# A float32 projection of the memory rows, and S5's input maps in three wide operations

## The chip, the cores and the metric

The kernel runs on one core of one Trainium2 chip. The metric is device time in microseconds (us) for one execution. Inputs, weights and outputs are float32 in HBM.

## What is computed

One inference step of a two-layer hybrid encoder, for a prompt of 512 tokens and a sample of 32 tokens, side by side as 544 columns of feature-major activations. Only the part around the change matters here:

```python
# memory rows, for both layers: 256 rows of width 1024
m = rms_norm(mem[None], mem_norm_g[:, None, None, :])
kv = jnp.einsum('lbmd,ldk->lbmk', m, w_mem_kv)          # (2 layers, 256 rows, 512)
k, v = jnp.split(kv, 2, axis=-1)
k = rms_norm(k.reshape(...), mem_k_norm_g[...])
# S5 (layer 0): discretised input matrix, then a complex diagonal recurrence per state
bb_re = f_re[..., None] * b_re - f_im[..., None] * b_im
bb_im = f_re[..., None] * b_im + f_im[..., None] * b_re
bu_re = jnp.einsum('blgc,gnc->blgn', ug, bb_re)
bu_im = jnp.einsum('blgc,gnc->blgn', ug, bb_im)
h_t = lam * h_(t-1) + bu_t                               # complex, by an associative scan
y = einsum(h_re, c_re) - einsum(h_im, c_im) + d_skip * u
```

Layer 0 then mixes S5 (with a gated linear unit, GLU) and attention into the memory rows, and a wide feed-forward network follows. Layer 1 has latent attention, memory attention and a second feed-forward network.

## The kernel before

**Matrix products.** Most products run in three terms of the reduced type fp32r: a float32 operand is split into a high part and a remainder, and hi*hi, hi*lo and lo*hi are summed in PSUM. `weights` makes the split of a weight block: SyncE's queue loads it into a slot `wraw` (three slots), ScalarE copies it to `whi` (L231) and its negative to `wlo` (L232), and a DMA issued by GpSimd adds the block from HBM onto `wlo` (L233). The activations are split by ScalarE (the copy) and VectorE (the remainder).

**Order.** The program is written in one order with a priority for each part (`ORDER`), and a planner, which runs a model of the engines, lays every engine's instructions out in a fixed order. A changed instruction can so move others.

**The stage of the change.** After the first product of layer 0 (`z0`, eight blocks, L324) the loop over `m` in 0..5 does S5 for eight groups of states at a time. In each turn:

- `s5_scan` (L752 to L782): products of the inputs with the maps `wv`, then the recurrence on VectorE;
- `s5_input` (L729 to L740): transposes of the next inputs, copied by ScalarE;
- `s5_wv` (L669, L672), in `products`: the input maps of the next `m`, on VectorE; `s5_wvt` (L681, L683), in `turn`: their transposes on TensorE and the copies on ScalarE;
- `s5_wc` (L694 to L710) and `s5_kernel` (L719): the output maps, and the short convolution kernel, which goes to DRAM (`kd`) and back by DMAs that GpSimd issues;
- `s5_output` (L791 to L805): true float32 products, transposes, and the activation.

`s5_wv` works on a real and an imaginary part. For each part it makes two products of 512 columns (L669) and one sum or difference of 512 (L672): six operations for each `m`.

**Memory rows.** `mem_kv` is a generator whose units the loop inserts with `fill` (priority `mem_kv`, -60: late). Eight units (four pairs of feature blocks, two layers) each scale and split two feature blocks (L344, L345), get a split weight block by `weights` from `w_mkv`, and issue twelve fp32r products of 128x512 (L350). The units after them make rms norms and transposes (L367 to L406) and stand at priority 580.

**Parameters of S5.** `s5_params` makes the powers `pr`, `pi` of the decay (L613 to L618), `bb` (L626 to L629), and by ScalarE the layouts `prd` (L654) and `xq` (L656).

Of the kernel before, what the change touches and what calls it, by code (L numbers as in the profile page):

```python
# [18 lines left out]
KD = D // 128  # L19
# [49 lines left out]
def view(a, dims, off=0):  # L69
    a = a[:]  # L70
    return bass.AP(tensor=a.tensor, offset=a.offset + off, ap=[a.ap[0]] + [list(d) for d in dims])
# [66 lines left out]
def body(ctx, tc, A, O):  # L138
# [7 lines left out]
    def slots(pool, n, dt, w, name):  # L146
        return Slots([pool.tile([128, w], dt, name=f"{name}{i}") for i in range(n)])
# [58 lines left out]
    def gcol(name, i):  # L206
        c = GP[name] + i
        return gp[:, c:c + 1]
# [18 lines left out]
    def weights(ap, *n, lo_eng=None):  # L227

        raw, hi, lo = WR.get(*n), WH.get(*n), WL.get(*n)
        nc.sync.dma_start(raw, ap)  # L230
        S.activation(hi, raw, AF.Copy)  # L231
        S.activation(lo, raw, AF.Copy, scale=-1.0)  # L232
        P.dma_start(lo, ap, accum_op=ALU.add)  # L233
        WR.put(raw)
        return hi, lo
# [8 lines left out]
    def wfree(w):  # L244
        WH.put(w[0])
        WL.put(w[1])
# [79 lines left out]
    def combos(a, b):  # L326
        return ((a[0], b[0]), (a[0], b[1]), (a[1], b[0]))
# [6 lines left out]
    def mem_kv(fm, rm, bm, b1, dst):  # L334
        ps = [[bm.get(512) for _ in range(2)] for _ in range(2)]
        acc = fm.get(2, NMEM)
        for u in range(4):
            mt = fm.get(2, NMEM)
            nc.sync.dma_start(mt, A["mem"][:, 2 * u:2 * u + 2, :])
            for l in range(2):  # L340
                hi, lo = rm.get(2, NMEM), rm.get(2, NMEM)
                for k2 in range(2):
                    g = gcol("mem", l * KD + 2 * u + k2)
                    S.activation(hi[:, k2], mt[:, k2], AF.Copy, scale=g)  # L344
                    V.scalar_tensor_tensor(lo[:, k2], mt[:, k2], g, hi[:, k2].bitcast(F32), ALU.mult, ALU.subtract)  # L345
                w = weights(A["w_mkv"][l, u], 1024, lo_eng=V if l else P)
                for t in range(2):
                    for k2 in range(2):
                        for i, (x, ww) in enumerate(combos((hi, lo), w)):
                            T.matmul(ps[l][t], x[:, k2, 128 * t:128 * t + 128], ww[:, 512 * k2:512 * k2 + 512],  # L350
                                     start=u == 0 and k2 == 0 and i == 0, stop=u == 3 and k2 == 1 and i == 2)
                wfree(w)
                rm.put(hi, lo)
                if l:
                    if u:
                        q = fm.get(2, NMEM)
                        S.activation(q, mt, AF.Square)
                        P.tensor_tensor(acc, acc, q, ALU.add)
                        fm.put(q)
                    else:  # L360
                        S.activation(acc, mt, AF.Square)
                    fm.put(mt)
                yield
        b = b1.get(512)
        for t in range(2):
            for u in range(2):
                T.matmul(b[:, t:t + 1], acc[:, u, 128 * t:128 * t + 128], ones, start=u == 0, stop=u == 1)  # L367
        x = sm(2, "mx", 1)
        V.tensor_scalar(x, b[:, :2], 1.0 / D, EPS, ALU.mult, ALU.add)
        b1.put(b)  # L370
        fm.put(acc)
        r = rsqrt(x, 128, 2, "mrs")
        yield
        for l in range(2):
            kt, v = dst[l]
            ss = sm(8, "mss")
            q = fm.get(2, 256)
            for t in range(2):
                S.activation(q[:, t], ps[l][t][:, :256], AF.Square, scale=r[:, t:t + 1])
                S.activation(v[:, t, :], ps[l][t][:, 256:], AF.Copy, scale=r[:, t:t + 1])  # L380
            V.tensor_reduce(ss, view(q, [[64, 8], [1, 64]]), AX.X, ALU.add)
            P.dma_start(O["mem_v"][l].rearrange("t p c -> p t c"), v)
            yield
            x = sm(8, "mkx")
            V.tensor_scalar(x, ss, 1.0 / 64, EPS, ALU.mult, ALU.add)
            y = rsqrt(x, 128, 8, "mkr")
            fm.put(q)
            V.tensor_tensor(y.rearrange("p (t h) -> p t h", t=2), y.rearrange("p (t h) -> p t h", t=2),
                            view(r, [[1, 2], [0, 4]]), ALU.mult)
            yield  # L390
            kk = fm.get(2, 256)
            for t in range(2):
                V.tensor_tensor(kk[:, t].rearrange("p (h d) -> p h d", d=64),
                                ps[l][t][:, :256].rearrange("p (h d) -> p h d", d=64),
                                view(y, [[1, 4], [0, 64]], 4 * t), ALU.mult)
            bm.put(*ps[l])
            kf = view(kk, [[64, 8], [1, 64]])
            V.tensor_tensor(kf, kf, view(grow(f"mk{l}"), [[0, 8], [1, 64]]), ALU.mult)
            P.dma_start(O["mem_k"][l].rearrange("t p c -> p t c"), kk)
            yield  # L400
            pt = b1.get(512)
            for hp in range(2):
                for t in range(2):
                    T.transpose(pt[:, 256 * hp + 128 * t:256 * hp + 128 * t + 128],
                                kk[:, t, 128 * hp:128 * hp + 128], ident)
            S.activation(kt.rearrange("p a b -> p (a b)"), pt, AF.Copy, scale=mqg[:, l:l + 1])  # L406
            b1.put(pt)
            fm.put(kk)
            yield
# [136 lines left out]

    def s5_params(pool, tmp, sp5):
        q = {}
        bb = pool.tile([128, 2, NPR, 16], F32, name="bb2")
        cc = pool.tile([128, 2, 48, 16], F32, name="cc2")  # L550
        braw = tmp[:, :2 * NPR * 16].rearrange("p (a b c) -> p a b c", a=2, b=NPR)
        nc.sync.dma_start(braw, A["s5b"])
# [67 lines left out]
        cm(3, 2, 2, 1)  # L620
        cm(5, 4, 4, 1)

        x, y = bb[:, 0], bb[:, 1]
        t = tmp[:, H:2 * H].rearrange("p (a b c) -> p a b c", a=2, b=NPR)
        frb, fib = view(fr, [[0, 2], [1, NPR], [0, 16]]), view(fi, [[0, 2], [1, NPR], [0, 16]])
        V.tensor_tensor(bb, braw, frb, ALU.mult)  # L626
        V.tensor_tensor(t, braw, fib, ALU.mult)
        V.tensor_tensor(x, x, t[:, 1], ALU.subtract)
        V.tensor_tensor(y, y, t[:, 0], ALU.add)  # L629

        tab = pool.tile([128, 2, NPR, 70], F32, name="tab")
        V.memset(tab[:, 0, :, 0:1], 1.0)
# [16 lines left out]
        for half in range(2):  # L649
            a = slice(64 * half, 64 * half + 64)  # L650
            for gh in range(2):
                c = slice(64 * gh, 64 * gh + 64)
                for i, src in enumerate((pr, pi)):
                    S.activation(view(prd[a], [[48, 9], [8, NM], [1, 4]], 432 * i + 4 * gh),  # L654
                                 view(src[c], [[NPR, 9], [4, NM], [1, 4]]), AF.Copy)
                S.activation(view(xq[a], [[128, NM], [1, 64]], 64 * gh),  # L656
                             view(bb[c], [[64, NM], [1, 64]], 16 * NPR * half), AF.Copy)
        q.update(pr=pr, pi=pi, bb=bb, cc=cc, tab=tab, prd=prd, xq=xq)
        q["kp"] = pool.tile([128, 2, 240], F32, name="kp")
        P.memset(q["kp"], 0.0)  # L660
        q["hf"] = pool.tile([128, NM, 8, 2], F32, name="hf")
# [1 line left out]

    def s5_wv(q, m, fa, fb):

        a, b = fa.get(2, 4, 128), fb.get(2, 4, 128)
        for ri in range(2):
            for o, x, pw in ((a, ri, "pr"), (b, 1 - ri, "pi")):
                V.tensor_tensor(o[:, ri].rearrange("p i (s c) -> p i s c", s=8),  # L669
                                view(q["bb"], [[16, 4], [0, 8], [1, 16]], 16 * (NPR * x + 4 * m)),  # L670
                                view(q[pw], [[1, 4], [NPR, 8], [0, 16]], 4 * m), ALU.mult)
            V.tensor_tensor(a[:, ri], a[:, ri], b[:, ri], ALU.add if ri else ALU.subtract)  # L672
        fb.put(b)
        return a

    def s5_wvt(a, fs, fd, bs):
        wv = []
        for ri in range(2):
            pb = bs.get(512)
            for i in range(4):  # L680
                T.transpose(pb[:, 128 * i:128 * i + 128], a[:, ri, i], ident)  # L681
            w = fs.get(4, 128)
            S.activation(w.rearrange("p a b -> p (a b)"), pb, AF.Copy)  # L683
            bs.put(pb)
            wv.append(w)
        fd.put(a)
        return wv
# [313 lines left out]
    exr.close()  # L1001
    exr = ExitStack()
    lr = exr.enter_context(tc.tile_pool(name="l0b", bufs=1, reuse_waits="tile"))
    R, fx = slots(lr, 4, F32R, 512, "rb"), slots(lr, 3, F32, FW, "fx")
    FA, FB, FD = slots(lr, 2, F32, 1024, "wv"), slots(lr, 1, F32, 2 * FW, "tb"), slots(lr, 3, F32, 2 * FW, "wc")
    fxs = list(fx.free)
    F.merge(fx)
# [793 lines left out]
```

## Time and profile before

| | |
|---|---|
| three runs | 1451.24, 1451.76, 1459.61 us (median 1451.76) |
| profiled execution | 1449.85 us, of which span 1448.1 us |
| busy share of the span | TensorE 97%, VectorE 50%, ScalarE 52%, GpSimd 27% |
| mean granted TensorE clock | 0.985 of full |

The span is the time from the first to the last instruction that the profiler records. Matmuls overlap in the pipeline and their ends are modelled, so the step from one start to the next, not the duration, is the price of a matmul; the same goes for VectorE, where an operation begins before the one ahead has drained. In an engine's timeline the brackets give the idle time ahead of an instruction and what ended it. The two shares say little of the change: the stage that it touches lasts about a tenth of the span.

### The profile page before, as it was taken

The numbers are of one execution on the slowest core, as the hardware profiler recorded it, in microseconds if no ns is written. First come the engines' busy times: TensorE is split into PE (matmuls) and PEld (weight loads), VectorE is DVE, ScalarE is ACT, GpSimd is POOL, SyncE is SP. The second block draws the span as 40 slices with busy tenths as digits, with TensorE's granted clock in tenths as the row PEclk, the third lists the DMA queues.
The fourth block names the chain that finished last, engine by engine and source line by source line (L and its number), as shares of the span: only waits on it lengthen the run. The fifth ranks groups of instructions, "written<-read, shape, count | busy, mean of one in ns | idle before, by whom it ended". The sixth has DMA issues, their size and how long they took to land.

```text
span 1448.1 us, 26899 instructions
## 1 busy us (share of the span) xinstructions
PE 1403.1 (97%) x10693; PEld 1310.7 (91%) x10693; DVE 723.6 (50%) x1810; ACT 755.9 (52%) x1247; POOL 388.6 (27%) x676
## 2 busy tenths in 40 slices
PE   7978799999999999999989999999999999999998
PEld 6966689999999999999988987557999999999998
DVE  7989742455514551455257655663355513551351
ACT  6656555565535553556555554654555534553452
POOL 2155432322111211124325421432322211221121
PEclk8999889999999999999999999999999999999999
DMA  9754637778788888869742432002778887888875
GB/s 268 163 142 121 155 75 175 169 164 175 176 179 171 176 176 178 173 141 207 158 120 62 124 102 60 11 20 57 165 171 177 177 175 172 176 177 174 176 157 139
DMA packets 67198, 214.80 MB, mean 148 GB/s; under 512 B 9280, under 2 KB 11552, under 8 KB 67072
## 3 DMA queue, kind: packets, MB, share of 16 engines
q0 software_dynamic: 30304, 100.81, 38.5%
q1 hardware_dynamic: 35616, 110.17, 26.5%
q10 hardware_dynamic: 1152, 2.10, 0.4%
q8 instruction: 84, 1.38, 0.4%
q14 instruction: 42, 0.34, 0.1%
HBM read 207.41 MB, written 5.61 MB: 147 GB/s over the span
## 4 chain that ended last, share of the span: by engine, by line
PE 82%; DVE 2%; DMA 2%; ACT 2%; issue 2%; POOL 1%; DVEq 0%; POOLq 0%; ACTq 0%
PE bank L324 64%; PE bank L1308 2%; PE bank L1556 2%; PE bank L1395 2%; PE bank L1592 1%; PE bank L1509 1%; PE bank L1483 1%; PE bank L1581 1%; DMA wlo<-i_w_f 1%; PE bank L1197 1%; PE bank L482 1%; PE bank L520 1%; PE bank L1423 1%; PE bank L510 0%; PE bank L1364 0%
## 5 line engine op out<-in xcount | busy, mean ns | idle before, releaser
L324 PE MATMUL bank<-rc,whi 128*128 128x272 f32 x3728 | 628.9, 290 | 0.2 <-DVE rc L305 0.2
L324 PEld LDWEIGHTS bank<-rc,whi 128*128 128x128 f32 x3728 | 530.3, 189 | 5.3 <-issue 4.3
L324 PE MATMUL bank<-rc,wlo 128*128 128x272 f32 x1864 | 389.4, 289 | 0.0
L231 ACT ACTIVATE whi<-wraw 128x1024 fp32r<-128x1024 f32 (+2 forms) x186 | 191.5, 1029 | 360.1 <-issue 311.3
L324 PEld LDWEIGHTS bank<-rc,wlo 128*128 128x128 f32 x1864 | 294.0, 189 | 0.4 <-issue 0.2
L324 PE MATMUL bank<-g,whi 128*128 128x272 f32 x1408 | 234.6, 288 | 0.8 <-ACT g L216 0.8
L324 PEld LDWEIGHTS bank<-g,whi 128*128 128x128 f32 x1408 | 198.8, 188 | 1.3 <-ACT g L216 1.2
L233 POOL DMA_DIRECT2D wlo<-i_w_f x136 | 117.5, 864 | 303.8 <-ACT wlo L232 300.5
L232 ACT ACTIVATE wlo<-wraw 128x1024 fp32r<-128x1024 f32 (+2 forms) x186 | 189.1, 1017 | 3.9 <-PE bank L350 3.3
L324 PE MATMUL bank<-g,wlo 128*128 128x272 f32 x704 | 145.8, 288 | 1.8 <-DMA wlo<-i_w_f 1.6
L851 DVE SCALAR_TENSOR_TENSOR fa<-fa,gp,fa 128x546 f32<-128x546 f32 x88 | 69.7, 792 | 139.8 <-ACT fa L850 139.8
L865 DVE TENSOR_TENSOR h<-bank,h 128x272 f32<-128x272 f32 x96 | 38.2, 436 | 172.3 <-PE bank L324 171.9
L324 PEld LDWEIGHTS bank<-g,wlo 128*128 128x128 f32 x704 | 110.4, 188 | 2.2 <-DMA wlo<-i_w_f 2.2
L850 ACT ACTIVATE fa<-fa,gp 128x546 f32<-128x546 f32 x88 | 73.2, 832 | 12.8 <-DVE fa L845 12.8
L843 DVE TENSOR_TENSOR fa<-bank,fa 128x272 f32<-128x272 f32 x88 | 38.9, 443 | 81.7 <-PE bank L324 77.5
L852 DVE SCALAR_TENSOR_TENSOR fa<-fa,gp,fa 128x546 f32<-128x546 f32 x88 | 69.5, 790 | 3.1
L891 ACT ACTIVATE fa<-fa 128x546 f32<-128x546 f32 x44 | 29.2, 663 | 71.7 <-DVE fa L852 71.7
L847 POOL COPY fa<-gp 128x2 f32<-128x2 f32 x88 | 19.0, 216 | 168.3 <-DVE g L217 107.7
L848 POOL COPY fa<-fa 128x4 f32<-128x4 f32 x88 | 18.2, 207 | 165.2 <-DVE fa L845 165.2
L324 PE MATMUL bank<-ra,whi 128*128 128x272 f32 x256 | 47.5, 307 | 3.1 <-ACT whi L241 3.1
L216 ACT ACTIVATE g<-fa 128x544 fp32r<-128x544 f32 x44 | 29.0, 659 | 37.6 <-DVE fa L893 37.6
L892 DVE TENSOR_TENSOR fa<-fa,fa 128x512 f32<-128x512 f32 x44 | 30.5, 693 | 33.6 <-ACT fa L891 33.6
(629 smaller groups left out, 2020.3 us busy)
## 6 DMA issues: line engine op xcount, KB each, us to landing
wraw<-i_w_f SPq DMA_DIRECT2D x120, 512.0 KB, 4.9
wlo<-i_w_f POOLq DMA_DIRECT2D x120, 512.0 KB, 7.4
wraw<-i_w_out SPq DMA_DIRECT2D x16, 512.0 KB, 4.3
wlo<-i_w_out POOLq DMA_DIRECT2D x16, 512.0 KB, 7.1
wraw<-i_w_in SPq DMA_DIRECT2D x14, 512.0 KB, 5.0
wlo<-i_w_in POOLq DMA_DIRECT2D x14, 512.0 KB, 7.7
wraw<-i_w_f SPq DMA_DIRECT2D x16, 384.0 KB, 3.4
wlo<-i_w_f POOLq DMA_DIRECT2D x16, 384.0 KB, 6.3
```

The source lines that it names most:

```text
L216: S.activation(hi, src, AF.Copy)
L231: S.activation(hi, raw, AF.Copy)
L232: S.activation(lo, raw, AF.Copy, scale=-1.0)
L233: P.dma_start(lo, ap, accum_op=ALU.add)
L324: T.matmul(ps[q][:, :c], ww, xx[:, c0:c0 + c], start=k == 0 and i == 0, stop=k == n - 1 and i == 2)
L843: V.tensor_tensor(u[:, 2:274], ps[0][:, :272], rb[:, :272], ALU.mult)
L850: S.activation(y, u[:, 2:548], AF.Identity, scale=gcol("cw", 3 * ci + 2), bias=gcol("cb", ci))
L851: V.scalar_tensor_tensor(y, u[:, 1:547], gcol("cw", 3 * ci + 1), y, ALU.mult, ALU.add)
L852: V.scalar_tensor_tensor(y, u[:, 0:546], gcol("cw", 3 * ci), y, ALU.mult, ALU.add)
L865: V.tensor_tensor(h[m][:, c0:c0 + cc], ps[qd][:, :cc], h[m][:, c0:c0 + cc], ALU.add)
L891: S.activation(yg, yg, AF.Silu)
L892: V.tensor_tensor(u[:, 2:514], ya[:, :NP], yg[:, :NP], ALU.mult)
```

## The change

The memory rows are no longer split: each unit loads the weight block, scales two feature blocks (L344's operation), and issues four true float32 products of 128x512 on the float32 data. L345, L231, L232 and L233 fall away there, and the slots `R` of this stage are two of float32 instead of four of fp32r.

S5's input maps are made for both parts at once. For that, `bb` is laid out state by state with real and imaginary part side by side, `bs` holds the same with the parts swapped, and `pr2`, `pi2` hold the powers twice (`pi2` with the first sign turned). ScalarE makes these by six copies in `s5_params`. `s5_wv` then is two products and a sum of 1024 columns.

```diff
@@ mem_kv
-                hi, lo = rm.get(2, NMEM), rm.get(2, NMEM)
+                x, w = rm.get(2, NMEM), WR.get(1024)
+                nc.sync.dma_start(w, A["w_mkv"][l, u])
                 for k2 in range(2):
-                    g = gcol("mem", l * KD + 2 * u + k2)
-                    S.activation(hi[:, k2], mt[:, k2], AF.Copy, scale=g)
-                    V.scalar_tensor_tensor(lo[:, k2], mt[:, k2], g, hi[:, k2].bitcast(F32), ALU.mult, ALU.subtract)
-                w = weights(A["w_mkv"][l, u], 1024, lo_eng=V if l else P)
+                    S.activation(x[:, k2], mt[:, k2], AF.Copy, scale=gcol("mem", l * KD + 2 * u + k2))
                 for t in range(2):
                     for k2 in range(2):
-                        for i, (x, ww) in enumerate(combos((hi, lo), w)):
-                            T.matmul(ps[l][t], x[:, k2, 128 * t:128 * t + 128], ww[:, 512 * k2:512 * k2 + 512],
-                                     start=u == 0 and k2 == 0 and i == 0, stop=u == 3 and k2 == 1 and i == 2)
-                wfree(w)
-                rm.put(hi, lo)
+                        T.matmul(ps[l][t], x[:, k2, 128 * t:128 * t + 128], w[:, 512 * k2:512 * k2 + 512],
+                                 start=u == 0 and k2 == 0, stop=u == 3 and k2 == 1)
+                WR.put(w)
+                rm.put(x)
@@ s5_params
-        bb = pool.tile([128, 2, NPR, 16], F32, name="bb2")
+        bb = pool.tile([128, NPR, 2, 16], F32, name="bb2")
+        bs = pool.tile([128, NPR, 2, 16], F32, name="bs2")
+        pr2 = pool.tile([128, 8, NPR, 2], F32, name="pr2")
+        pi2 = pool.tile([128, 8, NPR, 2], F32, name="pi2")
...
+        for o, src, s in ((view(pr2, [[2, 8 * NPR]]), pr, 1.0), (view(pr2, [[2, 8 * NPR]], 1), pr, 1.0),
+                          (view(pi2, [[2, 8 * NPR]]), pi, -1.0), (view(pi2, [[2, 8 * NPR]], 1), pi, 1.0)):
+            S.activation(o, view(src, [[1, 8 * NPR]]), AF.Copy, scale=s)
...
+        S.activation(bs[:, :, 0], y, AF.Copy)
+        S.activation(bs[:, :, 1], x, AF.Copy)
@@ s5_wv
-        a, b = fa.get(2, 4, 128), fb.get(2, 4, 128)
-        for ri in range(2):
-            for o, x, pw in ((a, ri, "pr"), (b, 1 - ri, "pi")):
-                V.tensor_tensor(o[:, ri].rearrange("p i (s c) -> p i s c", s=8),
-                                view(q["bb"], [[16, 4], [0, 8], [1, 16]], 16 * (NPR * x + 4 * m)),
-                                view(q[pw], [[1, 4], [NPR, 8], [0, 16]], 4 * m), ALU.mult)
-            V.tensor_tensor(a[:, ri], a[:, ri], b[:, ri], ALU.add if ri else ALU.subtract)
+        a, b = fa.get(8, 128), fb.get(8, 128)
+        for o, x, pw in ((a, "bb", "pr2"), (b, "bs", "pi2")):
+            V.tensor_tensor(o.rearrange("p i (s c) -> p i s c", s=8), view(q[x], [[16, 8], [0, 8], [1, 16]], 128 * m),
+                            view(q[pw], [[1, 8], [2 * NPR, 8], [0, 16]], 8 * m), ALU.mult)
+        V.tensor_tensor(a, a, b, ALU.add)
@@ s5_wvt
-                T.transpose(pb[:, 128 * i:128 * i + 128], a[:, ri, i], ident)
+                T.transpose(pb[:, 128 * i:128 * i + 128], a[:, 2 * i + ri], ident)
@@ body
-    R, fx = slots(lr, 4, F32R, 512, "rb"), slots(lr, 3, F32, FW, "fx")
+    R, fx = slots(lr, 2, F32, 512, "rb"), slots(lr, 3, F32, FW, "fx")
```

## Rows read from the trace of the kernel before

**Rows 1.** Busy time by stretch: PE, PEld, DVE, ACT, POOL, clock, DMA share, GB/s.

```profile
34.20:68.40 34.20, 34.20 (x277) 34.20 (x277) 33.27 (x87) 19.95 (x36) 4.29 (x5) 1.00 0.75 171
68.40:160.00 91.60, 74.60 (x714) 60.99 (x711) 84.54 (x156) 58.90 (x133) 51.01 (x90) 0.96 0.61 144
160.00:184.00 24.00, 17.80 (x84) 14.36 (x84) 12.92 (x50) 8.92 (x21) 7.63 (x12) 0.69 0.39 110
216.00:1448.10 1232.10, 1218.43 (x9267) 1151.05 (x9265) 554.10 (x1371) 624.56 (x973) 305.57 (x526) 1.00 0.67 147
```

**Rows 2.** Groups of VectorE instructions by line and shape, from 68.4 to 160.

```profile
L345 DVE SCALAR_TENSOR_TENSOR rb<-fa,gp,rb 128x256 fp32r<-128x256 f32 x12 | 6.7, 562 | 0.0
...
L345 DVE SCALAR_TENSOR_TENSOR rb<-big,gp,rb 128x256 fp32r<-128x256 f32 x4 | 1.9, 477 | 0.0
```

**Rows 3.** VectorE's timeline: start, duration, instruction.

```profile
60.53 1.35 DVE L694 TENSOR_TENSOR wc<-cc,prd 128x1152 f32<-128x1152 f32 x1
61.80 1.35 DVE L694 TENSOR_TENSOR tb<-cc,prd 128x1152 f32<-128x1152 f32 x1
...
65.63 0.69 DVE L669 TENSOR_TENSOR tb<-bb,pi 128x512 f32<-128x512 f32 x1
66.23 0.69 DVE L669 TENSOR_TENSOR wv<-bb,pr 128x512 f32<-128x512 f32 x1
...
91.05 0.48 DVE L345 SCALAR_TENSOR_TENSOR rb<-big,gp,rb 128x256 fp32r<-128x256 f32 x1
91.44 0.69 DVE L672 TENSOR_TENSOR wv<-wv,tb 128x512 f32<-128x512 f32 x1
```

**Rows 4.** TensorE's timeline: fp32r products (L350), true float32 products (L189, L791, L792).

```profile
1.52 3.78 PE L189 MATMUL bank<-fa 128*128 128x512 f32 x4 [1.52 <-DVE fa L185]
...
90.98 0.38 PE L792 MATMUL bank<-wc,fx 128*69 128x128 f32 x2
91.20 0.38 PE L791 MATMUL bank<-fa,fa 128*69 128x128 f32 x2
...
98.07 0.87 PE L350 MATMUL bank<-whi,rb 128*128 128x512 f32 x3
98.78 0.40 PE L350 MATMUL bank<-wlo,rb 128*128 128x512 f32 x1
```

**Rows 5.** Timeline: VectorE's longest wait in the stage, and ScalarE before its end.

```profile
99.62 1.05 ACT L231 ACTIVATE whi<-wraw 128x1024 fp32r<-128x1024 f32 x1
...
100.57 0.58 ACT L683 ACTIVATE fa<-bank 128x512 f32<-128x512 f32 x1
...
102.11 0.45 DVE L763 TENSOR_TENSOR fa<-bank,tab 128x276 f32<-128x276 f32 x1 [5.38 <-ACT wlo L232]
```

**Rows 6.** ScalarE's timeline in the parameter stage.

```profile
43.11 0.38 ACT L654 ACTIVATE prd<-pr 64x216 f32<-64x216 f32 x1
43.40 0.37 ACT L654 ACTIVATE prd<-pi 64x216 f32<-64x216 f32 x1
43.79 2.13 ACT L656 ACTIVATE xq<-bb 64x384 f32<-64x384 f32 x4
...
47.64 1.04 ACT L232 ACTIVATE wlo<-wraw 128x1024 fp32r<-128x1024 f32 x1
```

**Rows 7.** Timelines of GpSimd and TensorE: that block's remainder, issued and first used.

```profile
48.98 0.86 POOL L233 DMA_DIRECT2D wlo<-i_w_in  x1 [9.79 <-ACT wlo L232]
...
58.31 0.41 PE L324 MATMUL bank<-ra,wlo 128*128 128x272 f32 x2
```

**Rows 8.** Instructions of one tensor (`i_w_in`, 46 to 56): time from issue to landing.

```profile
DMA to landing us min/median/max: 6.7/7.1/7.5
```

**Rows 9.** Waits of SyncE's queue, 36 to 160: us in total, times, longest.

```profile
SPq L230 <- ACT wlo L232: 56.4, 9, 10.2
SPq L339 <- DVE fa L773: 20.4, 1, 20.4
```

**Rows 10.** Instructions of one line (L707, GpSimd): shortest, median, longest in ns.

```profile
L707 POOL TENSOR_TENSOR kp<-kp,fa x5: 406/562/1539, 72.7 to 136.6; 128x32 f32<-128x32 f32 x5
```

More of the change, by code (lines that the diff above doesn't have):

```diff
@@ L621, in s5_params @@
         cm(5, 4, 4, 1)
-        x, y = bb[:, 0], bb[:, 1]
+        for o, src, s in ((view(pr2, [[2, 8 * NPR]]), pr, 1.0), (view(pr2, [[2, 8 * NPR]], 1), pr, 1.0),
+                          (view(pi2, [[2, 8 * NPR]]), pi, -1.0), (view(pi2, [[2, 8 * NPR]], 1), pi, 1.0)):
+            S.activation(o, view(src, [[1, 8 * NPR]]), AF.Copy, scale=s)
+        x, y = bb[:, :, 0], bb[:, :, 1]
         t = tmp[:, H:2 * H].rearrange("p (a b c) -> p a b c", a=2, b=NPR)
         frb, fib = view(fr, [[0, 2], [1, NPR], [0, 16]]), view(fi, [[0, 2], [1, NPR], [0, 16]])
-        V.tensor_tensor(bb, braw, frb, ALU.mult)
+        V.tensor_tensor(view(bb, [[16, 2], [32, NPR], [1, 16]]), braw, frb, ALU.mult)
         V.tensor_tensor(t, braw, fib, ALU.mult)
@@ L655, in s5_params @@
                                  view(src[c], [[NPR, 9], [4, NM], [1, 4]]), AF.Copy)
-                S.activation(view(xq[a], [[128, NM], [1, 64]], 64 * gh),
-                             view(bb[c], [[64, NM], [1, 64]], 16 * NPR * half), AF.Copy)
-        q.update(pr=pr, pi=pi, bb=bb, cc=cc, tab=tab, prd=prd, xq=xq)
+                S.activation(view(xq[a], [[128, NM], [16, 4], [1, 16]], 64 * gh),
+                             view(bb[c], [[128, NM], [32, 4], [1, 16]], 16 * half), AF.Copy)
+        q.update(pr2=pr2, pi2=pi2, bb=bb, bs=bs, cc=cc, tab=tab, prd=prd, xq=xq)
         q["kp"] = pool.tile([128, 2, 240], F32, name="kp")
```

## The prediction

> **What bounds the kernel now.** I read the table of busy time by stretch first, since the page's shares are a mean over unlike stages [rows 1]. From 216 us to the end TensorE is busy for 1218.4 of 1232.1 us at full clock: whatever is won or lost before 216 arrives at the end unchanged, and nothing behind it can be won by this change. From 34.2 to 68.4 TensorE is busy throughout (the z0 products). In the S5 stage, 68.4 to 160, the picture turns: VectorE is busy for 84.5 of 91.6 us (92%), TensorE for 74.6 (81%), ScalarE for 58.9, GpSimd for 51.0. There the time is VectorE's, with waits of the chain around it. From 160 to 184 nothing is full (TensorE 17.8 of 24.0 at a mean clock of 0.69): this is the tail of S5's last outputs and of the memory keys, latency after latency. Then I read VectorE's groups in the S5 stage and its timeline, for what the change takes from it and at what step [rows 2, 3], TensorE's timeline for the two kinds of product [rows 4], and the one long gap of VectorE [rows 5].
>
> **The change part by part.**
>
> *VectorE, memory rows.* The 16 remainders L345 go [rows 2]. One costs the step to the next start, 91.44 - 91.05 = 0.39 us [rows 3]; 16 x 0.39 = 6.2 us, all inside the stretch where VectorE is 92% busy. (Their durations sum to 8.6 us, since some were stretched; I don't count that.)
>
> *VectorE, input maps.* Columns have a slope and each operation a fixed part. A 512-column product steps 0.60 us (65.63 to 66.23), a 1152-column one 1.27 (60.53 to 61.80) [rows 3]: slope 0.67/640 = 1.05 ns a column, fixed part 0.60 - 0.54 = 0.06 us. Three of 1024 cost 3 x (1.07 + 0.06) = 3.4 us for each m against 6 x 0.60 = 3.6; over six m 1.3 us less. The two-operand layouts keep an innermost run of 16, so I take the slope as it is. Between no gain (0) and the fixed part of 18 removed operations at the 0.07 that rounding allows (1.3), I take 1.3.
>
> A rule speaks against it. The trace shows a GpSimd addition, L707, that lasts from 0.41 to 1.54 us [rows 10]. The Trainium skill, "SBUF — State Buffer", section "Who interferes with whom", says that a VectorE operation with two SBUF inputs and a GpSimd operation that reads SBUF shut each other out for a whole instruction. By that rule a wider operation could hold each of the six additions longer by 1.13 - 0.60 = 0.53 us, 3.2 us in all if every one met it and lay on the path; the sum below leaves this at nothing, as the range of L707 does not tell what stretched it.
>
> *TensorE.* 96 fp32r products of 512 columns become 32 true float32 ones. A fp32r one steps (98.78 - 98.07)/3 = 0.237 us. A true float32 one of 128 columns (recorded as two) steps 91.20 - 90.98 = 0.22 us [rows 4]; times four for 512 columns, 0.88. The nearest by shape is the pair of 128x512 at the start, 3.78 us for two, 1.9 each [rows 4], with the engine fresh from idle; 0.88 is half of it. I take 0.88, since the stage runs at 0.96 of full clock [rows 1]. 32 x 0.88 - 96 x 0.237 = 28.2 - 22.8 = +5.4 us of TensorE. At the price of the start it would be +38 us, far from the clock of this stage; that end belongs to a stage that falls to the lower of the two levels, 1.2 instead of 2.4 GHz.
>
> A rule speaks against it too: the Trainium skill, "FP8 and Floating Point Precision", section "TensorE Precision Notes", says that true FP32 takes four passes. Against three fp32r terms that is a third more TensorE work; from the measured 22.8 us it would be +7.6 (an estimate from that page) where rows give +5.4.
>
> *ScalarE.* Eight pairs L231, L232 go: 16 x 0.95 (the step 99.62 to 100.57 [rows 5]) = 15.2 us of an engine that is 64% busy in the stage. That is mostly cover already; where it is not, one case shows: VectorE's gap of 5.4 us before 102.11 ends when the scan's products arrive, behind the copy L683, which stood behind L231 for 0.95 us [rows 5]. I take 1.0 us; bounds 0 and the whole gap, 5.4.
>
> *ScalarE, new copies.* Four copies of 192 columns at no more than the 0.29 step of 216 columns, and two of 384 at 0.53 (2.13/4) [rows 6]: 2.2 us, in a place where ScalarE works without a break, ahead of the weight split that ends at 48.68 [rows 6]. Its DMA is issued at 48.98 and lands 6.7 to 7.5 us later [rows 7, 8]; the first product with that remainder starts at 58.31 [rows 7]. 48.98 + 7.5 + 2.2 = 58.7: worst case +0.4, taken 0. VectorE's first maps now wait for these copies; they are used at 68.4, 26 us behind, so 0; if that cover failed, 2.2.
>
> *GpSimd and DMA.* Eight issues L233 of 0.86 us [rows 7] and their accumulating DMA go: 6.9 us of GpSimd, where the round trips of `kd` are issued. No gain taken.
>
> *SyncE's queue.* Here a wait is moved. A slot `wraw` was free behind L232; now it is held until TensorE has used it. The queue waits 56.4 us for L232 already, the longest 10.2; behind such a wait stand the loads of the memory rows (L339), one of which itself waits 20.4 us for a data slot [rows 9], and GLU's first weights. Three slots run ahead of units that are filler, so I take 0; if that cover is gone once, a load is late by its landing, at most the 7.5 us of the slowest [rows 8].
>
> **The sum.** VectorE loses 6.2 + 1.3 = 7.5 us, and 1.0 of a wait. Next late is TensorE: 74.6 + 5.4 = 80.0 us of work in a stage that would be 91.6 - 8.5 = 83.1 long, 96% busy with a fixed order and many hops to ScalarE and back. I let it run as full as VectorE runs now, 92%: 80.0/0.923 = 86.7 us. That is later than VectorE's 83.1, so it sets the stage: 91.6 - 86.7 = 4.9 us gained. The tail and all behind move along. 1448.1 - 4.9 = 1443.2 span, with the 1.75 around it 1444.95; the median of the runs stands 1.9 above the profiled execution, so **1446.9**. With TensorE at the 96%, the gain is 8.5 (1443.3); with none of TensorE's 5.4 covered it is 3.1 (1448.7).
>
> **The rivals.**
> *More than the sum.* If VectorE's whole gap of 5.4 closes with its 7.5 gone, the stage loses 12.9: 1438.9. If the tail (24 us with TensorE 6.2 idle and at 0.69 clock) also closes by some us, since the memory keys no longer wait for split weights, about 1435. For it: ScalarE and GpSimd both get lighter exactly there. Against: TensorE's load would reach 80.0/78.7, more than the stage holds, unless its work moves into the tail.
> *No change.* The extra TensorE work and its waits eat the whole of VectorE's relief: 1450 to 1453. For it: gains of an engine at 92% were never fully on the chain.
> *Slower, by blocking.* A filler product now holds TensorE for 0.88 us instead of 0.24. If the fixed order puts one ahead of each hop TensorE-ScalarE-TensorE (transposes, scan, maps, outputs: six a turn, 36 in all), each waits (0.88 - 0.24)/2 = 0.32 us longer: 11.5 us, less the 4.9: +6.6, 1458.4. It decides once the added waits exceed the relief, at about 15 of the 36 hops. The same result comes by keeping TensorE at its present 81%: 80.0/0.814 = 98.2, +6.6. For it: TensorE is in order and the stage is a chain. Against: the units are at low priority, and the planner can place them in waits that TensorE has anyway, 17.0 us of the 91.6.
> *It does not do what it says*, a compiled order or memory layout that moves other waits at random: this widens every case by some 2 us rather than being one of its own.
>
> **How the numbers follow.** Forecast (gain 3 to 9) 0.45; more than the sum (gain 9 to 18) 0.24; no change (within 3) 0.17; slower by blocking (3 to 12) 0.14. The forecast's own range is 1443 to 1449. For 8 in 10 I go down to 1436, into the first rival's tail, and up to 1456, through most of the last. One per cent, 14.5 us, is about what a measurement of this kernel tells from no change; beyond it lie only the far end of the first rival (0.13) and the far end of the last with a fall of the clock (0.04).
>
> **What would show it.** L345 and the mkv rows of L231 to L233 gone; VectorE's busy time in the S5 stage down from 84.5 to about 77; three steps of about 1.13 us for each m; product steps of 0.88 at full clock; TensorE's share of the stage above 90%, and the GLU products starting about 5 us before 184. The prediction is wrong if the float32 products cost another step, if the stage stays as long with VectorE idle behind TensorE, or if the tail from 160 to 184 changes by more than the stage does.

## The result, and the profile after

The changed kernel takes 1438.42 us (median of five runs, 1436.17 to 1441.98) against 1453.32 for the kernel before on the same chip (1451.24 to 1459.61): ratio 0.9891, 95% interval 0.986 to 0.9923. The span of its profiled execution is 1434.4 us, 13.7 less than before. The forecast was 1446.9, a gain of 4.9, with 1443 to 1449 as its own range; what came is the rival "more than the sum".

Busy time by stretch after, columns as in [rows 1]:

```profile
34.20:68.40 34.20, 34.20 (x273) 34.03 (x274) 33.45 (x82) 17.20 (x37) 2.57 (x3) 1.00 0.55 122
68.40:160.00 91.60, 82.39 (x705) 58.24 (x704) 84.10 (x149) 48.07 (x123) 54.50 (x91) 0.94 0.43 118
160.00:184.00 24.00, 23.86 (x146) 18.81 (x145) 12.23 (x49) 13.72 (x36) 4.45 (x9) 0.88 0.36 106
216.00:1434.40 1218.40, 1204.37 (x9170) 1138.71 (x9168) 546.72 (x1364) 614.64 (x958) 303.31 (x524) 1.00 0.67 147
```

Beside [rows 1], TensorE in the S5 stretch went from 74.6 to 82.4 us, and the stretch from 160 to 184 is full where it was three quarters full: the GLU products have moved into it. VectorE's 84.1 looks like no relief at all, but the stretch is a fixed window and work that used to lie behind 160 is now inside. For the length of the stage one has to take marks that move with it: VectorE's six scans, one for each `m`, and the first GLU product. VectorE's timeline, first and last scan, before:

```profile
75.35 1.31 DVE L770 TENSOR_TENSOR_SCAN fx<-fa,fa 128x560 f32<-128x560 f32 x1
...
154.55 1.32 DVE L770 TENSOR_TENSOR_SCAN big<-big,fx 128x560 f32<-128x560 f32 x1
```

and after:

```profile
65.29 1.23 DVE L674 TENSOR_TENSOR wv<-bb,pr 128x1024 f32<-128x1024 f32 x1 [0.33 <-PE bank L324]
66.44 1.22 DVE L674 TENSOR_TENSOR tb<-bs,pi 128x1024 f32<-128x1024 f32 x1
67.57 1.35 DVE L698 TENSOR_TENSOR wc<-cc,prd 128x1152 f32<-128x1152 f32 x1
...
76.23 1.31 DVE L774 TENSOR_TENSOR_SCAN fx<-fa,fa 128x560 f32<-128x560 f32 x1
...
145.32 1.31 DVE L774 TENSOR_TENSOR_SCAN big<-big,fx 128x560 f32<-128x560 f32 x1
```

From first to last scan it was 79.2 us and is 69.1: 10.1 less. VectorE's idle time between the two scans, summed from the brackets of the timeline, fell from 6.3 to 2.3 us: 4.0 of the 10.1. The rest is work that VectorE no longer has. The first three lines also show the wide operations, at steps of 1.15 and 1.13 us.

Then TensorE's timeline at the end of S5, before:

```profile
175.45 3.57 PE L430 MATMUL bank<-cn,fa 128*128 128x2 f32 x16 [0.78 <-ACT fa L406]
...
184.01 0.82 PE L324 MATMUL bank<-rc,whi 128*128 128x272 f32 x2
```

and after, with the float32 products ahead of it:

```profile
75.39 1.02 PE L347 MATMUL bank<-wraw,rb 128*128 128x512 f32 x2
76.34 0.88 PE L756 MATMUL bank<-big,fa 128*64 128x69 f32 x21
...
159.65 1.92 PE L347 MATMUL bank<-wraw,rb 128*128 128x512 f32 x2
161.35 0.63 PE L796 MATMUL bank<-wc,fa 128*69 128x128 f32 x2
...
165.81 1.05 PE L427 MATMUL bank<-cn,fa 128*128 128x2 f32 x8
166.79 0.70 PE L479 MATMUL bank<-fa,fa 64*128 64x256 f32 x4
167.43 1.05 PE L427 MATMUL bank<-cn,fa 128*128 128x2 f32 x8
...
171.38 0.82 PE L324 MATMUL bank<-rc,whi 128*128 128x272 f32 x2
```

The first GLU product starts at 171.38 instead of 184.01, 12.6 earlier. From the marks: the first scan is 0.9 later, the scans take 10.1 less, and from the last scan to GLU it is 26.1 instead of 29.5, 3.4 less. A later mark, which every kernel passes with the whole of this stage behind it, is the first remainder of the feed-forward network's input (L305). On VectorE's timeline, before:

```profile
274.55 4.71 DVE L305 SCALAR_TENSOR_TENSOR rc<-h,gp,rc 128x544 fp32r<-128x544 f32 x5 [2.37 <-ACT rc L304]
```

after:

```profile
261.07 4.71 DVE L305 SCALAR_TENSOR_TENSOR rc<-h,gp,rc 128x544 fp32r<-128x544 f32 x5 [2.37 <-ACT rc L304]
```

It comes 13.5 us earlier, and from there to the end it is 1173.5 us before and 1173.3 after: the gain is won ahead of it and arrives unchanged. The sixteen small products of memory attention (L430 before, L427 after) take 3.57 us before and 2.10 after: the granted clock was 0.56 from 171 to 184 before, the lower of the two levels for most of it, and 0.88 from 163 to 171.4 after.

### The profile page after: what moved, and what is told of

The parts are those of the page before. It is cut to its first block, busy times and chain, and to the rows that moved or that the text cites. A ratio compares the mean times of both kernels' runs of the same rounds, so it can differ in the third digit from the quotient of the medians.

```text
span 1434.4 us, 26764 instructions
## 1 busy us (share of the span) xinstructions
PE 1402.3 (98%) x10661; PEld 1299.2 (91%) x10661; DVE 714.6 (50%) x1776; ACT 740.6 (52%) x1237; POOL 385.7 (27%) x668
## 4 chain that ended last, share of the span: by engine, by line
PE 87%; DMA 4%; DVE 3%; ACT 2%; issue 2%; POOL 1%; SPq 0%; ACTq 0%; DVEq 0%; POOLq 0%
PE bank L324 67%; PE bank L1312 2%; PE bank L1560 2%; PE bank L1399 2%; PE bank L1596 1%; DMA wlo<-i_w_in 1%; PE bank L1513 1%; PE bank L1487 1%; PE bank L1585 1%; PE bank L347 1%; DMA wlo<-i_w_f 1%; PE bank L1201 1%; PE bank L479 1%; PE bank L1427 1%; PE bank L517 1%
## 5 line engine op out<-in xcount | busy, mean ns | idle before, releaser
L231 ACT ACTIVATE whi<-wraw 128x1024 fp32r<-128x1024 f32 (+2 forms) x178 | 182.9, 1028 | 354.3 <-issue 304.0
L233 POOL DMA_DIRECT2D wlo<-i_w_f x136 | 116.7, 858 | 303.9 <-ACT wlo L232 302.5
L232 ACT ACTIVATE wlo<-wraw 128x1024 fp32r<-128x1024 f32 (+2 forms) x178 | 180.6, 1015 | 0.6 <-PE bank L1513 0.5
```

## The experiments

Twelve kernels were run. All times are medians; each ratio is to the kernel before on the same chip (1452.0, 1452.3, 1453.7 and 1452.3 in the four groups, 1453.3 for the changed kernel). A difference of two medians from different groups so has an uncertainty of a few us. "Scans" is the time from first to last scan, "idle" VectorE's idle time in it, and "mark" the start of L305, all read from the timeline of the profiled execution as above.

| kernel | us | ratio to before (95%) | scans | idle | mark |
|---|---|---|---|---|---|
| before | 1452 to 1454 | 1 | 79.2 | 6.3 | 274.6 |
| changed | 1438.42 | 0.9891 (0.986, 0.9923) | 69.1 | 2.3 | 261.1 |
| mem_only | 1438.07 | 0.989 (0.9852, 0.9928) | 74.6 | 6.5 | 260.6 |
| s5_only | 1461.85 | 1.0059 (1.0038, 1.008) | 91.3 | 20.4 | 283.4 |
| split_back | 1435.52 | 0.9876 (0.9842, 0.9909) | 72.5 | 5.3 | 261.3 |
| rem_back | 1438.52 | 0.9899 (0.9862, 0.9936) | 73.2 | 1.1 | 265.4 |
| late_weights | 1442.68 | 0.9934 (0.9907, 0.9962) | 74.3 | 7.0 | 264.8 |
| late_both | 1446.21 | 0.995 (0.9926, 0.9973) | 78.7 | 6.2 | 267.8 |
| three_hi | 1432.50 | 0.987 (0.984, 0.9899) | 68.5 | 2.9 | 257.0 |
| three_weights | 1445.62 | 0.9944 (0.9925, 0.9964) | 78.9 | 12.7 | 269.7 |
| three_rows | 1452.49 | 0.9985 (0.9959, 1.0012) | 84.5 | 14.3 | 273.5 |
| one_pass | 1437.25 | 0.9893 (0.9873, 0.9913) | 71.4 | 6.2 | 260.3 |
| before_m60 | 1456.57 | 1.0023 (1.0002, 1.0045) | 91.4 | 17.5 | 278.9 |
| s5_kp_dve | 1446.23 | 0.9955 (0.9938, 0.9971) | 79.5 | 8.2 | 267.8 |

The mark is of one execution, and orders the kernels nearly as the time does. What lies behind it differs by a few us more from kernel to kernel (1170 to 1177 us of span), so a difference is trusted here where mark and time agree.

### The two parts by themselves, and unused work put back

**mem_only** is the float32 projection alone, **s5_only** the three wide operations alone: each kernel takes the one part of the diff and leaves the other as before.

> The float32 projection of the memory rows alone; S5's input maps stay at six operations of 512 columns. Theory A (VectorE's relief shortens the S5 stage, 6.2 us of it from the remainders L345, 1.3 from the wide maps; the tail follows because the memory keys come earlier): nearly all of the gain is here, 12 to 14 us below the kernel before. Theory B (what counts is the data path: eight split weight blocks fewer on ScalarE, GpSimd and the DMA queues, so that the round trips of kd are short): the same, 12 to 15. Theory C (the gain is the planner's new order, any edit moves the tail by several us): anywhere between 0 and 20 below.

> The three wide operations for S5's input maps alone; the memory rows stay split. Theory A: 1 to 2 us below the kernel before (18 operations' fixed part). Theory B: 0 to 1 us below. Theory C: several us in either direction, with the tail (last S5 output to the first GLU product, 13.6 us before) at another length.

The projection alone gives the whole gain, 1438.07. It doesn't come in the same place as in the changed kernel: the scans take only 4.6 us less than before, with VectorE's idle time as before, and from the last scan to GLU it is 22.0 us instead of 29.5. The wide operations alone lose about 9 us, where the prediction had counted a gain of 1.3; on top of the projection they cost nothing (1438.42).

**split_back** and **rem_back** put the removed work back into the changed kernel without using it:

```diff
 split_back
+                wh, wl = WH.get(1024), WL.get(1024)
+                S.activation(wh, w, AF.Copy)
+                S.activation(wl, w, AF.Copy, scale=-1.0)
+                P.dma_start(wl, A["w_mkv"][l, u], accum_op=ALU.add)
+                wfree((wh, wl))
 rem_back, in the loop over k2
+                    V.scalar_tensor_tensor(lo[:, k2], mt[:, k2], g, x[:, k2], ALU.mult, ALU.subtract)
```

> The changed kernel, with the split of the eight weight blocks made again but used by nobody (two ScalarE copies of 1024 columns and the accumulating DMA by GpSimd, each). Theory A: within 3 us of the changed kernel (12 to 15 below the kernel before), as ScalarE and GpSimd have room. Theory B: most of the gain is gone, 0 to 6 below the kernel before, and GpSimd waits for kd's way to DRAM more than 15 us again, instead of 8.7. Theory C: anything.

> The changed kernel, with the 16 remainders of the memory rows made again on VectorE but used by nobody. Theory A: 6 us of the gain are gone in the S5 stage: 7 to 10 below the kernel before. Theory B: within 2 us of the changed kernel, 13 to 15 below. Theory C: anything.

Neither gives the gain back. The copies, the GpSimd issues and the DMA traffic, unused, cost nothing (mark 261.3, 1435.5). The sixteen remainders on VectorE, the main term of the forecast, delay the mark by 4.4 us (265.4), of which the median shows nothing (1438.5): at most a third of the gain. So most of it is not shown to be work that an engine was relieved of. What is common to the kernels at 1435 to 1438 and missing from those above 1450 is that no product waits for a remainder.

### Waits put back, form put back

**late_weights** keeps float32 products and makes each weight block take the way of the old remainder; **late_both** makes the rows wait for VectorE as well. The values stay as they were.

```diff
 late_weights
                 nc.sync.dma_start(w, A["w_mkv"][l, u])
+                S.activation(w, w, AF.Copy, scale=0.0)
+                P.dma_start(w, A["w_mkv"][l, u], accum_op=ALU.add)
 late_both, also
+                    V.scalar_tensor_tensor(x[:, k2], mt[:, k2], g, x[:, k2], ALU.mult, ALU.min)
```

> The changed kernel, but each weight block of the memory rows first passes the old path: ScalarE writes it times zero over itself, and a DMA issued by GpSimd adds the block from HBM. The true float32 products use what this leaves, so the values are the same and nothing is left out. Theory 'dependency' (the float32 form gains because a product needs nothing but the loaded block, while the split made it wait for a copy and a DMA of some 7 us): the gain goes, 1447 to 1455. Theory 'form' (four long float32 products in place of twelve short ones, whatever they wait for): the gain stays, 1435 to 1441. Splitting alone, unused, cost nothing (1435.5), so traffic is no reason for a third result.

> True float32 products that wait for all that the split's products waited for: the weights by ScalarE's copy and the accumulating DMA, as in the kernel with late weights (1442.7), and the rows by an added VectorE operation of 256 columns for each block, which takes the lesser of the product and ScalarE's copy of it and so leaves the values as they are. Theory 'dependency': 1447 to 1455, most of the gain is gone. Theory 'form': it stays at 1440 to 1444, and the split's products are slow for what they are.

With the waits put back the time is 4.3 and then 7.8 us more than the changed kernel's (1442.7, 1446.2; at the mark 3.7 and 6.7), though the products keep their form. The interval of late_weights overlaps that of the changed kernel, so its 4.3 is not clear of noise; in late_both the added VectorE work has its part. It comes 3.0 us behind late_weights at the mark, no more than the sixteen remainders cost that nobody uses (4.4), so with float32 products a price for the rows' wait itself is not shown. The first came out between the two ranges, the second just under the range of "dependency" and above that of "form". So the waits are at most one part of the answer for these products, and not all of the way back to 1452.

**three_hi** goes the other way: the old twelve fp32r products, and nothing to wait for but one copy. **three_rows** and **three_weights** add one of the two remainders, and s5_only has both.

```diff
 three_hi (against the changed kernel)
+                S.activation(wh, w, AF.Copy)
...
+                        for i in range(3):
+                            T.matmul(ps[l][t], x[:, k2, 128 * t:128 * t + 128], wh[:, 512 * k2:512 * k2 + 512], ...)
 three_rows (against s5_only; wh is ScalarE's copy of the block, no wlo is made)
...
-                        for i, (x, ww) in enumerate(combos((hi, lo), w)):
+                        for i, (x, ww) in enumerate(((hi, wh), (hi, wh), (lo, wh))):
 three_weights (against s5_only; no lo of the rows is made)
...
-                        for i, (x, ww) in enumerate(combos((hi, lo), w)):
+                        for i, (x, ww) in enumerate(((hi, w[0]), (hi, w[1]), (hi, w[0]))):
```

> The changed kernel, but each unit of the memory rows again issues twelve fp32r products of 128x512, all three of a term on the high parts (ScalarE rounds the block and the rows; no remainder is made, no accumulating DMA). It leaves out the two remainder terms of the memory projection. TensorE has its old 22.8 us there. Theory 'dependency': 1435 to 1441, as with float32. Theory 'form': 1450 to 1462, as in the two kernels that had twelve products.

> Between the kernel with twelve products on high parts (1432.5) and the one with the three wide operations alone (1461.9), which differ only in the remainders: here the remainder of the rows is made by VectorE and used, and the weights are taken as their high part in all three terms (it leaves out the term with the remainder of the weights). Theory 'row remainder' (products wait for VectorE, the busiest engine): 1448 to 1462. Theory 'weight remainder' (products wait for the second copy and the accumulating DMA): 1431 to 1440.

> The other half: the weights' remainder is made by copy and accumulating DMA and used, the rows are taken as their high part in all three terms (it leaves out the term with the remainder of the rows). Theory 'weight remainder': 1448 to 1462. Theory 'row remainder': 1431 to 1440. If each half gives about 1447, both waits count alike and add.

This is the clearest result of the study. With the same 96 products: no remainder 1432.5, the weights' remainder 1445.6 (+13.1), the rows' remainder 1452.5 (+20.0), both 1461.85 (+29.4); at the mark +12.7, +16.5 and +26.4. The medians are from three chips; by the ratios the differences are some 10.7, 16.7 and 27.4. "Form" falls: twelve short products that wait for nothing but copies are no slower than the float32 ones. By the medians they are 5.9 us faster (4.1 at the mark), but the two intervals overlap, so the size of that is not shown. Both remainders count, the rows' (made by VectorE, the fullest engine) for more.

How much of that is VectorE's added work follows from the table. Between the scans three_rows is 16.0 us longer than three_hi, and 11.4 of it is idle time of VectorE; for three_weights it is 10.4 and 9.8, for s5_only 22.8 and 17.5. So the remainders on VectorE take some 5 us there as work, and the larger part is VectorE waiting. Two things are not separated: three_hi with remainders that nobody uses was not run, and three_rows and three_weights have four slots for the rows where three_hi has two.

Where it costs can be seen in three_rows. VectorE's timeline:

```profile
108.87 1.22 DVE L682 TENSOR_TENSOR wv<-wv,tb 128x1024 f32<-128x1024 f32 x1
...
111.67 1.35 DVE L704 TENSOR_TENSOR tb<-cc,prd 128x1152 f32<-128x1152 f32 x1
118.17 0.45 DVE L773 TENSOR_TENSOR fa<-bank,tab 128x276 f32<-128x276 f32 x1 [5.14 <-ACT whi L348]
```

and TensorE's in that time:

```profile
113.50 0.79 PE L739 MATMUL bank<-cn,fa 128*69 128x128 f32 x4 [0.78 <-ACT fa L815]
114.04 1.42 PE L353 MATMUL bank<-whi,rb 128*128 128x512 f32 x5
115.30 0.71 PE L691 MATMUL bank<-cn,wv 128*128 128x128 f32 x5
115.76 0.48 PE L353 MATMUL bank<-whi,rb 128*128 128x512 f32 x1
116.08 0.49 PE L691 MATMUL bank<-cn,wv 128*128 128x128 f32 x3
116.33 0.71 PE L353 MATMUL bank<-whi,rb 128*128 128x512 f32 x2
117.35 1.19 PE L762 MATMUL bank<-fx,fa 128*64 128x69 f32 x32 [0.31 <-ACT fa L693]
```

VectorE idles for 5.1 us until the scan products L762 are there. Those need the transposes L691 of the maps `wv`, which VectorE had finished at about 110. But L691, which starts at 115.30, stands in TensorE's order behind outputs, two products of the memory rows, L739, which waits for ScalarE, and five products of the memory rows (L353), which take 1.3 us. The releaser that the row of VectorE names, a ScalarE copy L348, makes no operand of L762 or L773. The waits of the products themselves for the rows' remainder come to 0.9 us in the whole stage. So neither those waits nor the products that stand ahead are most of the 5.1 us. TensorE came to this place late, and the rows ahead of it, on GpSimd, VectorE, ScalarE and TensorE, show why:

```profile
102.66 3.38 POOL L717 TENSOR_TENSOR kp<-kp,fa 128x32 f32<-128x32 f32 x1 [6.95 <-ACT kp L716]
102.67 0.46 DVE L345 SCALAR_TENSOR_TENSOR rb<-fa,gp,rb 128x256 fp32r<-128x256 f32 x1
106.07 0.38 ACT L741 ACTIVATE fa<-bank 69x256 f32<-69x256 f32 x1 [2.90 <-POOL kp L717]
107.14 0.69 PE L749 MATMUL bank<-cn,fa 69*128 69x69 f32 x4 [2.98 <-ACT fa L741]
```

An addition of 32 columns on GpSimd lasts 3.38 us; ScalarE's copy of the next inputs waits 2.90 us for it and TensorE's transposes 2.98 us for the copy. VectorE works without a break in that time, and a remainder L345 is the first of its operations there. TensorE's granted clock was 1.00 from 97 to 103.9; then, behind the idle time, columns as in [rows 1]:

```profile
107.10:113.50 6.40, 5.58 (x28) 4.78 (x28) 5.89 (x7) 4.30 (x12) 4.57 (x10) 0.54 0.50 144
```

So the outputs and products ahead of L691 ran near the lower of the two levels. At full clock and with a wait of 0.31 us, as in three_hi, TensorE would have been at L691 some 5.6 us earlier (an estimate: 2.98 - 0.31, and 6.4 x 0.46), which is about when its operands were ready. There the addition at this place (98.30) took 0.45 us, and the clock stayed at 1.00 from 97 to 115. The other long wait of VectorE in three_rows, 5.38 us, ends at 137.42; ahead of it stand an addition of 3.62 us (124.49) and a wait of TensorE of 3.22 us (129.12). In three_weights no addition lasts more than 1.03 us. There ScalarE's copy of the inputs waits 8.8 us in three because the addition itself starts late, behind other work in GpSimd's order; GpSimd waits 18.8 us for the way of `kd` to DRAM, and 7.2 in three_hi (11.0 in split_back, where it cost nothing).

What the traces show is thus a chain: GpSimd's addition late or long, ScalarE's copy behind it, TensorE idle and then at the lower clock, and at its end VectorE. Why a remainder leads to it, by being waited for, by its place in the laid-out order or by running beside the addition, is not shown. The gap of 5.4 us in the kernel before [rows 5] has filler in its way too, seven L350 ahead of L681, which take 1.7 us. In three_hi VectorE's longest wait between the scans is 2.4 us.

**one_pass** is three_hi with one product in place of three.

> The same with one fp32r product in place of three: 7.6 us of TensorE for the memory rows in place of some 28. It leaves out the remainder terms. Theory 'length' (TensorE's added work keeps its clock up through the tail and that is the gain): slower than the changed kernel, 1443 to 1452, with a lower clock from 150 to 190. Theory 'dependency': 1432 to 1440. The forecast's own step (TensorE's load sets the stage at 92 per cent): 20 us less of TensorE is worth up to 7 us until VectorE sets the stage, 1429 to 1434.

1437.25: the dependency theory's range. "Length" falls, and so does the forecast's own step, by which 20 us less of TensorE should have been worth up to 7. It is no faster than three_hi with 15 us less to do, but 4.8 us slower in the median and 3.3 at the mark. The S5 stretch of one_pass:

```profile
68.40:160.00 91.60, 71.20 (x684) 59.19 (x683) 84.60 (x155) 57.35 (x136) 54.32 (x92) 0.85 0.48 125
```

and of three_hi:

```profile
68.40:160.00 91.60, 79.37 (x772) 65.45 (x771) 86.89 (x161) 60.98 (x145) 55.69 (x93) 0.99 0.49 131
```

TensorE at 71.2 us busy was granted 0.85 of its clock, at 79.4 us busy 0.99.

**before_m60** is the kernel before with another order of the same work.

```diff
-ORDER = {..., "mem_kv": -60, ...
+ORDER = {..., "mem_kv": 60, ...
```

> The kernel before with one number changed: the units of the memory rows stand at priority +60 in place of -60, so the planner lays the same instructions in another order. Theory 'order' (the change gained by the order that the planner came to, above all by memory keys that are done earlier): some of the gain comes without the change, 1438 to 1447. Otherwise, 1449 to 1458: the order of the same work is worth a few us either way and the form of the work is what counts.

1456.6: the scans take 91.4 us instead of 79.2, and a shorter way from the last scan to GLU (18.8 instead of 29.5) doesn't make up for it. This one other order of the same products does not give the gain; others were not tried.

### The wide operations

Why does s5_only lose 9 us? GpSimd's timeline in it:

```profile
104.83 3.36 POOL L714 TENSOR_TENSOR kp<-kp,fa 128x32 f32<-128x32 f32 x1 [1.68 <-ACT kp L713]
```

VectorE's at that time:

```profile
104.83 0.46 DVE L345 SCALAR_TENSOR_TENSOR rb<-fa,gp,rb 128x256 fp32r<-128x256 f32 x1
105.21 1.39 DVE L780 TENSOR_TENSOR fa<-fx,tab 128x560 f32<-128x560 f32 x2
106.51 1.22 DVE L677 TENSOR_TENSOR wv<-bb,pr 128x1024 f32<-128x1024 f32 x1
107.65 0.43 DVE L786 TENSOR_TENSOR fa<-fa,fa 64x280 f32<-64x280 f32 x1
```

and ScalarE's behind it:

```profile
108.23 0.38 ACT L738 ACTIVATE fa<-bank 69x256 f32<-69x256 f32 x1 [2.90 <-POOL kp L714]
```

An addition of 32 columns lasts 3.36 us while VectorE runs two-operand operations without a break; ScalarE's copy L738 of the next inputs waits 2.9 us for it, and TensorE's transposes L746 wait 3.0 for the copy. Over the stage ScalarE's L738 waits 8.9 us for L714. In VectorE's unbroken run stand both a remainder (L345) and a wide product (L677). This is the rule that the prediction weighed, the Trainium skill's "SBUF — State Buffer", section "Who interferes with whom"; the trace agrees with it here. The prediction had priced it at 0.53 us for each addition, the growth of one operation; here an addition is held for a run of several, and its median is 2.27 us where it was 0.56 before [rows 10]. **s5_kp_dve** takes the addition off GpSimd:

```diff
-            P.tensor_tensor(kp[:, :, 112:128], kp[:, :, 112:128], dd, ALU.add)
+            V.tensor_tensor(kp[:, :, 112:128], kp[:, :, 112:128], dd, ALU.add)
```

> The kernel with the three wide operations alone (1461.9, 8 to 9 us slower than before), with GpSimd's addition of the skip term onto kp done by VectorE instead, same operands and result. In that kernel's trace the addition lasted 2.27 us in the median and 3.36 at most, while VectorE ran two-operand operations without a break, and ScalarE's copy of the next inputs waited for it 8.9 us in three waits. Theory 'exclusion' (the stretched GpSimd operation is what the wide operations cost): 1450 to 1456. Theory 'order' (the planner's order around wide operations, the addition only shares the wait): 1458 to 1464.

1446.23, 15.6 us faster than s5_only: more than the 9 that the wide operations had cost, and below the expected range. All instructions of the line, s5_only first (shortest, median, longest in ns):

```profile
L714 POOL TENSOR_TENSOR kp<-kp,fa x5: 244/2272/3362, 72.7 to 146.3; 128x32 f32<-128x32 f32 x5
```

then s5_kp_dve, on VectorE:

```profile
L714 DVE TENSOR_TENSOR kp<-kp,fa x5: 180/181/193, 73.6 to 139.2; 128x32 f32<-128x32 f32 x5
```

and the changed kernel, where ScalarE waits 2.9 us for it in three times:

```profile
L711 POOL TENSOR_TENSOR kp<-kp,fa x5: 421/647/1194, 73.1 to 129.5; 128x32 f32<-128x32 f32 x5
```

So taking this addition off GpSimd gives back all that s5_only had lost, and more. The planner's order changed with it in part, so that the exclusion alone is worth all of the 15.6 is not shown. It is also a place through which the remainders cost time, as the rows of three_rows show: the longest addition was 3.62 us there and 1.24 in three_hi. In the kernel before, though, ScalarE waits only 3.4 us for the addition over the stage, and 2.9 in the changed kernel, so between these two little changed there. The same edit to the kernel before and to the changed kernel was not run, so how much of the 29.4 us goes through this one addition, and how much of the change's gain could be had without the change by moving it, stays open.

## Why the prediction was right or wrong

**The reading of the bound** held in part. All behind the mark moved along. But that the S5 stage's time "is VectorE's" was a third of it: rem_back, which gives VectorE its sixteen remainders back, is 4.4 us later at the mark and no later in the median.

**VectorE's terms.** The step of the wide operations is 1.13 to 1.15 us for the 1.13 worked out. The sum of 7.5 us of relief shows as 6.1 us between the scans (10.1 less 4.0 of idle time), and by rem_back it is worth 4.4 us at the mark and nothing that the medians show. The 1.3 us for the wide operations had the wrong sign where it stands alone: +9 in s5_only, 0 beside float32 products. The rule against it, priced at 3.2 us and left at nothing, was the more important part there.

**TensorE's term** was near. A float32 product, recorded as two, steps 0.95 us at 75.39 (forecast 0.88; the lower clock level gives 1.7 at 159.65). Added up over the two traces, without idle time, the 32 products take some 32 us and the 96 took some 28: 4 more, where the sum had 5.4 and the other price that the prediction named was 7.6. What that work costs in end time is not settled by changed kernel and three_hi (5.9 by the medians, with intervals that overlap).

**The step that failed** is the price of the waits, together with the cap and the tail. For the waits that fall away the prediction took 1.0 us, read off one copy (ScalarE's L231 ahead of L683), with 0 to 5.4 as bounds, and "no gain taken" for GpSimd and DMA; the tail was to move along, and a cap took 3.6 us off. In the traces of before and after, at the mark 13.5 us apart, VectorE's work between the scans gave 6.1 us, its idle time 4.0, the way from the last scan to GLU 3.4 and the way from there to the mark 0.8, less 0.9 for a first scan that came later. So the sum was short by about 3 us each for the waits, the tail and the cap. The split is that of these two traces: mem_only has the same gain with more of it behind the last scan.

The prediction asked for each engine how much work it loses. The experiments show that waiting can count for more: with twelve products the two remainders cost 29.4 us by the medians, in the surroundings of s5_only, of which some 5 is VectorE's work between the scans. With four float32 products the waits that were put back cost 7.8 us at most (late_both), the added VectorE work included. Where the traces let one follow it, this goes through GpSimd's addition, ScalarE's copy and TensorE's clock, and hardly through waits of the products themselves; which waits made up the change's own 4.0 and 3.4 us stays open. Along the path s5_only, three_hi, changed kernel the change is: wide operations +9, no remainders -29.4, float32 +5.9, together -14 to -15; by mem_only the wide operations are worth nothing, so this is one path and not a price list.

**The cap** of TensorE at 92% took 8.5 us of relief down to 4.9. Between the first and the last scan of the changed kernel TensorE is busy for 64.85 of 69.09 us, 94%, columns as in [rows 1]:

```profile
76.23:145.32 69.09, 64.85 (x567) 45.28 (x567) 66.39 (x102) 37.51 (x96) 44.48 (x74) 0.98 0.42 120
```

And in one_pass TensorE loses 20 us more and 1.2 us is gained, with the granted clock at 0.85. So the 92% was no cap.

**The tail** "moves along" was off by 3.4 us; the first rival had named this, and VectorE's gap (6.3 to 2.3 us of idle time). Of its two reasons, memory keys that no longer wait for split weights and lighter ScalarE and GpSimd, split_back speaks against the second: it gives that work back and loses nothing. That the time came out where this rival put it does not confirm its gap of 5.4 us closing as a whole.

**What was taken as nothing.** SyncE's queue now waits for TensorE as said, the longest wait of the first row of after 17.1 us:

```profile
SPq L342 <- PE bank L347: 37.7, 3, 17.1
...
SPq L339 <- DVE tab L649: 9.2, 1, 9.2
```

but the loads of the memory rows (L339) wait at most 9.2 us where one waited 20.4 [rows 9]: the cover held. What ScalarE's new copies cost can't be told from the first scan, 0.9 us later than before, with the order changed around it. "Slower, by blocking" did not come with float32 products. s5_only (+9) and before_m60 (+4) are as slow as it had said or nearly so, but for s5_only the addition on GpSimd was found behind it, and for before_m60 no cause was tested.

## What to carry to other kernels

In a stage that is a chain over several engines with filler between, ask of a change what each instruction will no longer have to wait for, as well as how much work each engine loses: here the removed work, put back unused, cost 0 and at most 4 us, and where its results were used up to 29. The list of waits does not show that price under the name of the instructions that changed. Take the longest waits of the fullest engine instead, and follow each back, from what is waited for to what that had waited for, with the clock beside it. A tiny operation that others wait for is best kept off GpSimd beside a VectorE that never pauses.

## What the runs showed of the hardware

- GpSimd's addition of 128x32 took from 0.24 to 3.36 us in one kernel (s5_only), the long ones beside unbroken two-operand operations of VectorE, several to one addition; the same on VectorE took 0.18.
- A wait of TensorE of 2.98 us was followed by a granted clock of 0.54 over the next 6.4 us (three_rows); where it waited 0.31 us at the same place the clock stayed at 1.00 (three_hi).
- Less work on TensorE went with a lower granted clock: 0.85 in the S5 stretch of one_pass (71.2 us busy) against 0.99 in three_hi (79.4 us), and the kernel with 15 us more to do was 4.8 us faster by the medians (3.3 at the mark).
- A true float32 product of 128x512 steps 0.86 to 1.0 us near full clock (0.95 at 75.39) and 1.7 at the lower level; at the start of the kernel it lasted 1.9 [rows 4], with the granted clock at 1.00 there, which no run explains.
